# First layer of a hybrid decoder trunk: rows split in fp16 halves and transposed by DMA, and the first loop's order written out for four engines

## The chip, the cores and the metric

The kernel runs on one core of a Trainium2 chip. A time is the device time of one execution in microseconds (us). The kernel before has three such times, and one more execution was recorded by the profiler; all rows below and in the prediction are from that recording.

## The reference, cut to what matters

The program computes two residual layers over 2048 tokens of width 1024. Layer 0, which the change is in, mixes by gated linear attention (4 heads, a state per head that runs along the sequence); layer 1 mixes by dilated windows. Both also attend to a memory of 256 tokens.

```python
def reference(x, mem, mem_norm_w, norm_w, w_memkv, w_out, w_in_a, w_gate_up, b_gate,
              gla_norm_w, w_in_b, final_norm_w):
    mem_n = rmsnorm(mem, mem_norm_w)
    for i in range(DEPTH):                       # DEPTH = 2
        h = rmsnorm(x, norm_w[i])
        j = i // N_MIXERS
        if i % N_MIXERS == 0:
            mix, q_mem, gate = gla_mixer(h, w_in_a[j], w_gate_up[j], b_gate[j], gla_norm_w[j])
        else:
            mix, q_mem, gate = dilated_mixer(h, w_in_b[j])
        mem_o = memory_attention(q_mem, mem_n, w_memkv[i])
        branch = jnp.concatenate([mix, mem_o], axis=-1) * jax.nn.silu(gate)
        x = x + branch @ w_out[i]
    return rmsnorm(x, final_norm_w)
```

`gla_mixer` projects `h` to q, k (384 columns each), v (768), a gate of rank 16, the memory query (256) and the branch gate (1024).

## The kernel before, in words

The 2048 tokens are 16 blocks of 128 rows (`NB` = 16). A matrix product in f32 accuracy is made from fp16 halves: each operand is split into hi and lo = value - hi, and `mm3` (L181, L182, L183) adds hi*hi, hi*lo and lo*hi. `proj` runs `mm3` over 8 tiles of 128 along the width of 1024, so 24 matmuls for each 256 columns. The weight-like side has to have the width in its partitions, so each block of rows is first transposed.

The first layer has two loops over the 16 blocks, one after the other.

- **First loop** (pools of the context `c1`). `ga(b)` loads block b of x (L365), squares it for the norm (L160), scales it (L379), transposes its 8 tiles of 128x128 on TensorE (`split_T`, L168), and writes the result into `hT` as halves: hi by ScalarE (L384), lo by VectorE (L385), each in two pieces of 512 columns. `hT` is also stored to DRAM (`hT_d`, L388), since the second loop needs it again. `pre_a` to `pre_d` project block b to v, the gate and q, k and turn the gate into decays by exponentials; `gla1` transposes k and q (L525, L530), copies them to `kT` and `qT` on ScalarE (L527, L532) and makes the matrix A of the block (L538, masked at L540); `gla2` makes the outputs and the new state S, and stores the block to `og_d` (L571). At b = 1 the loop also writes the memory's rows, norm, transposes, keys and values of both layers (`mem_kv`); at b = 2 to 6 it loads and splits five weight tiles that the second loop needs (`load_w256`: load L136, conversion L140).
- **Second loop** (context `c2`). `a2_q` reads `hT` back (L637), projects the memory query and attends to the memory; `a2_gate` projects the 1024 gate columns and applies silu into `sg`; `a2_branch` reads `og` back (L663), multiplies into `sg` (L664, L666), transposes `sg` by `split_T`, and writes the halves to `bT` (L672, L673); `a2_out` multiplies `bT` by w_out's four tiles `wo0` to `wo3` and adds the residual (x1 is stored at L691); `a2_h2` makes the norm of the second layer, its halves in `stg` (L701, L702) and, for most blocks, transposes them by one DMA (`h2T<-stg`, L703). At a few blocks, `SUMS_AT`, `a2_sums` makes extra sums for the second layer (L719 to L732). Between the loops w_out's tiles are loaded, scaled and split (`load_w`, with `norm_scale` L113 to L124).

What sets the order: the program's text is handed to a scheduler, which puts every engine's instructions in an order of its own by a model of their costs. Each engine then runs its list in that order, and an instruction that must wait holds back all behind it on its engine. All loads, stores and DMA transposes are issued by SyncE (`SY`), so they too form one list, in which an issue that waits for its input holds back the issues behind it. A tile name has as many buffers as its pool says: `k1` has two of each name, `k2` one.

Of the kernel before, what the change touches and what calls it, by code (L numbers as in the profile page):

```python
# [16 lines left out]
P = 128  # L17
T = 2048
D = 1024
KT = 8  # L20
# [16 lines left out]
def trunk(ctx, tc, a, out):  # L37
# [318 lines left out]
    with ExitStack() as c1:  # L356
# [17 lines left out]
        def ga(b):  # L374
# [3 lines left out]
            r = rstd_of(rowss(xt, k2), 1, D)  # L378
# [11 lines left out]

        wv2, iv2 = lw1(1280, 272, s1)
        hs = [ga(0)]
        xts[1] = load_x(1)
        hs.append(ga(1))
# [48 lines left out]
        def pre_a(b, hT):  # L443
            v = tl(k1, [P, 768], F32, "v")
            p0 = bank(ps_mm)
            proj(p0[:, :272], hT, wv2, 0, 272)
            gl = gls[b % 2]
# [4 lines left out]
            A.activation(out=v[:, 512:768], in_=p0[:, :256], func=AF.Copy, scale=iv2)  # L452
            t = bank(ps_tr)
            PE.transpose(t[:96, :P], gl.bitcast(F32), ident)
            glT = tl(k2, [96, P], F32R, "glT")
            V.tensor_copy(glT, t[:96, :P])
            z = bank(ps_g)
            PE.matmul(z[:, :384], glT, wgu, start=True, stop=True)
            la = tl(k2, [P, 384], F32, "la")
# [4 lines left out]
                                   op1=ALU.subtract)  # L464
            bb = bank(ps_g)
            lah = tl(k2, [P, 384], F32R, "lah")
            lal = tl(k2, [P, 384], F32R, "lal")
            A.activation(out=lah, in_=la, func=AF.Copy)
            V.tensor_tensor(out=lal, in0=la, in1=lah.bitcast(F32), op=ALU.subtract)
            PE.matmul(bb[:, :384], tri, lah, start=True, stop=False)  # L470
            PE.matmul(bb[:, :384], tri, lal, start=False, stop=True)
            eb = tl(k1, [P, 384], F32, "eb")
            enb = tl(k1, [P, 384], F32, "enb")
            elb = tl(k1, [P, 384], F32, "elb")
            A.activation(out=enb, in_=bb[:, :384], func=AF.Exp, scale=-1.0)
            A.activation(out=eb, in_=bb[:, :384], func=AF.Exp)
            br = bank(ps_g)
            PE.matmul(br[:, :384], rev, lah, start=True, stop=False)
            PE.matmul(br[:, :384], rev, lal, start=False, stop=True)
            for h in range(HA):  # L480
                PE.matmul(br[:DK, 384 + 2 * h:386 + 2 * h], la[:, h * DK:(h + 1) * DK], ind, start=True, stop=True)
            A.activation(out=elb, in_=br[:, :384], func=AF.Exp)
            dec = tl(k1, [DK, 8], F32, "dec")
            A.activation(out=dec, in_=br[:DK, 384:392], func=AF.Exp)
            return hT, (v, eb, enb, elb, dec)

        def pre_b(hT, r):
            v = r[0]
            p1 = bank(ps_mm)
            proj(p1[:, 0:256], hT, wv0, 0, 256)  # L490
            A.activation(out=v[:, 0:256], in_=p1[:, 0:256], func=AF.Copy, scale=iv0)  # L491
            proj(p1[:, 256:512], hT, wv1, 0, 256)
            A.activation(out=v[:, 256:512], in_=p1[:, 256:512], func=AF.Copy, scale=iv1)
# [4 lines left out]
        def pre_c(hT, r):  # L498
            v, eb, enb, elb, dec = r
            p2 = bank(ps_mm)  # L500
            proj(p2[:, 0:256], hT, wk1, 0, 256)
            scaled(enb[:, 128:384], p2[:, 0:256], ik1)
            scaled(elb[:, 128:384], p2[:, 0:256], ik1)

        def pre_d(hT, r):
            v, eb, enb, elb, dec = r
            p3 = bank(ps_mm)
            proj(p3[:, 256:512], hT, wqk, 0, 256)
            scaled(enb[:, 0:128], p3[:, 384:512], iqk)
# [65 lines left out]
        for b in range(2):  # L575
            pres[b] = pre_a(b, hs[b])
# [1257 lines left out]
```

## Time and profile before

| | |
|---|---|
| median of 3 runs | 2574.38 us (2570.02 to 2577.67) |
| the profiled execution | 2568.94 us, its span 2567.2 us, granted clock 0.993 |
| TensorE busy (PE) | 2489.6 us, 97% of the span, 17033 matmuls |
| VectorE (DVE), ScalarE (ACT), GpSimd (POOL) busy | 1579.0, 1345.7, 579.2 us |
| share of the chain that ended last | PE 79%, DVE 6%, DMA 5%, issue 4%, ACT 4%, POOL 2% |

The span is the recorded part of one execution, from its first to its last instruction; what lies around it is 1.7 us here. "Busy" is summed over instructions of one engine, and PE's weight loads (PEld) run beside its matmuls. The chain that ended last is followed back from the last instruction through what each one waited for. In the trace the first layer's first loop runs from about 60 to 440 us, the second loop from about 500 to 912 us, and the rest, to the end, is the second layer.

### The profile page before, as it was taken

The numbers are of one execution on the slowest core, as the hardware profiler recorded it, in microseconds if no ns is written. First come the engines' busy times: TensorE is split into PE (matmuls) and PEld (weight loads), VectorE is DVE, ScalarE is ACT, GpSimd is POOL, SyncE is SP. The second block draws the span as 40 slices with busy tenths as digits, with TensorE's granted clock in tenths as the row PEclk, the third lists the DMA queues.
The fourth block names the chain that finished last, engine by engine and source line by source line (L and its number), as shares of the span: only waits on it lengthen the run. The fifth ranks groups of instructions, "written<-read, shape, count | busy, mean of one in ns | idle before, by whom it ended". The sixth has DMA issues, their size and how long they took to land.

```text
span 2567.2 us, 45017 instructions
## 1 busy us (share of the span) xinstructions
PE 2489.6 (97%) x17033; PEld 1673.3 (65%) x17033; DVE 1579.0 (62%) x3582; ACT 1345.7 (52%) x2944; POOL 579.2 (23%) x471
## 2 busy tenths in 40 slices
PE   7989999899999999999999999999999999998999
PEld 6979999788889844444444445555555555554898
DVE  7446444665776765756555455577676767768643
ACT  7346543644454544756555456565565656555322
POOL 0000000010210223454543112233232323323100
PEclk9999999999999999999999999999999999999999
DMA  6242111434544554567675323457474765648752
GB/s 213 84 133 95 54 67 52 133 112 110 163 133 128 146 185 121 143 165 185 169 183 141 127 56 92 114 149 175 121 183 125 174 150 147 177 116 219 234 179 101
DMA packets 563311, 356.55 MB, mean 139 GB/s; under 512 B 383554, under 2 KB 495636, under 8 KB 562708
## 3 DMA queue, kind: packets, MB, share of 16 engines
q1 hardware_dynamic: 563092, 353.66, 50.2%
q8 instruction: 133, 2.18, 0.3%
q14 instruction: 86, 0.70, 0.1%
HBM read 185.74 MB, written 95.86 MB: 110 GB/s over the span
## 4 chain that ended last, share of the span: by engine, by line
PE 79%; DVE 6%; DMA 5%; issue 4%; ACT 4%; POOL 2%; SPq 1%; DVEq 0%; POOLq 0%; ACTq 0%
PE ps_mm L181 15%; PE ps_mm L183 15%; PE ps_mm L182 15%; PE ps_x L181 6%; PE ps_x L182 6%; PE ps_x L183 6%; DMA mpt<-stg 1%; PE ps_o L183 1%; PE ps_o L181 1%; PE ps_o L182 1%; PE ps_g L181 1%; PE ps_g L182 1%; PE ps_g L183 1%; DMA h2T<-stg 1%; PE ps_tr L168 1%
## 5 line engine op out<-in xcount | busy, mean ns | idle before, releaser
L181 PE MATMUL ps_mm<-h2T,w 128*128 128x512 f16 x1112 | 422.9, 380 | 5.9 <-ACT w L851 4.9
L183 PE MATMUL ps_mm<-h2T,w 128*128 128x512 f16 x1112 | 422.6, 380 | 0.3 <-DVE w L855 0.3
L182 PE MATMUL ps_mm<-h2T,w 128*128 128x512 f16 x1112 | 422.7, 380 | 0.0
L181 PE MATMUL ps_mm<-w,hT 128*128 128x256 f16 (+1 forms) x1408 | 387.3, 275 | 3.2 <-ACT v L491 1.2
L182 PE MATMUL ps_mm<-w,hT 128*128 128x256 f16 (+1 forms) x1408 | 386.2, 275 | 0.0
L183 PE MATMUL ps_mm<-w,hT 128*128 128x256 f16 (+1 forms) x1408 | 385.0, 275 | 0.4 <-DVE hT L385 0.4
L183 PEld LDWEIGHTS <-w 128*128 128x128 f16 x1952 | 191.5, 98 | 233.2 <-issue 3.0
L181 PEld LDWEIGHTS <-w 128*128 128x128 f16 x1952 | 191.6, 98 | 216.7 <-ACT w L851 5.0
L182 PEld LDWEIGHTS <-w 128*128 128x128 f16 x1952 | 191.5, 98 | 216.4 <-issue 9.0
L175 POOL TENSOR_TENSOR ph<-pm,ph 128x512 f16<-128x512 f32 (+2 forms) x144 | 163.1, 1132 | 630.8 <-ACT ph L174 433.0
L181 PE MATMUL ps_x<-h2T,w 128*128 128x512 f16 x552 | 209.9, 380 | 1.4 <-DVE c L1079 1.4
L182 PE MATMUL ps_x<-h2T,w 128*128 128x512 f16 x552 | 210.0, 380 | 0.0
L183 PE MATMUL ps_x<-h2T,w 128*128 128x512 f16 x552 | 209.8, 380 | 0.0
L1268 ACT ACTIVATE pm<-pm,st,cols 128x256 f32<-128x256 f32 (+1 forms) x288 | 156.1, 543 | 73.8 <-DVE st L1261 73.1
L175 POOL TENSOR_TENSOR stg<-mp,stg 128x512 f16<-128x512 f32 x16 | 18.6, 1161 | 742.3 <-DMA ogd<-og 457.5
L181 PEld LDWEIGHTS <-hT 128*128 128x128 f16 x1408 | 138.7, 99 | 24.2 <-issue 5.5
L1257 DVE CUSTOM_DVE_ANT_0 pm<-ps_g,mw 128x256 f32<-128x256 f32 (+1 forms) x288 | 93.0, 359 | 99.6 <-PE ps_g L183 99.0
L182 PEld LDWEIGHTS <-hT 128*128 128x128 f16 x1408 | 138.7, 98 | 23.0 <-issue 4.4
L183 PEld LDWEIGHTS <-hT 128*128 128x128 f16 x1408 | 139.2, 99 | 17.9 <-DVE hT L385 0.7
L1217 ACT ACTIVATE rx<-rw 128x512 f16<-128x512 f32 x36 | 33.8, 940 | 114.8 <-DVE rw L1216 114.8
L1201 ACT ACTIVATE rx<-ps_mm 32x512 f32<-32x512 f32 x96 | 56.1, 584 | 57.8 <-PE ps_mm L183 24.6
L174 ACT ACTIVATE ph<-pm 128x512 f16<-128x512 f32 (+2 forms) x144 | 77.3, 537 | 4.5
(593 smaller groups left out, 5982.4 us busy)
## 6 DMA issues: line engine op xcount, KB each, us to landing
stg<-in_w_in_b SPq DMA_DIRECT2D x80, 256.0 KB
v<-vd SPq DMA_DIRECT2D x72, 256.0 KB
fb<-fd SPq DMA_DIRECT2D x24, 768.0 KB
od<-osb SPq DMA_DIRECT2D x68, 256.0 KB
og<-od SPq DMA_DIRECT2D x68, 256.0 KB
x<-in_x SPq DMA_DIRECT2D x32, 512.0 KB
stg<-in_w_in_b SPq DMA_DIRECT2D x24, 512.0 KB
vd<-vo SPq DMA_DIRECT2D x48, 256.0 KB
```

What stands on the lines that cost most here:

```text
L168: PE.transpose(t[:, (k - k0) * P:(k - k0 + 1) * P], src[:, k * P:(k + 1) * P], ident)
L174: A.activation(out=hi, in_=src, func=AF.Copy)
L175: G.tensor_tensor(out=lo, in0=src, in1=hi, op=ALU.subtract)
L181: PE.matmul(o, sh, mh, start=first, stop=False)
L182: PE.matmul(o, sh, ml, start=False, stop=False)
L183: PE.matmul(o, sl, mh, start=False, stop=last)
L1201: A.activation(out=X[r0:r0 + 32, :], in_=t[0:32, :], func=AF.Copy)
L1217: A.activation(out=fold(X.bitcast(F16)[:, 0:512], g), in_=perm(W, g), func=AF.Copy, scale=SQ)
L1257: V.tensor_tensor_reduce(out=pm[:, at:at + w * P], in0=s[:, at:at + w * P], in1=masks["mw" if w == 2 else "mf"], scale=1.0, scalar=NEG, op ...
L1268: A.activation(out=p_, in_=p_, func=AF.Exp, scale=sc, bias=st[:, jc + jj:jc + jj + 1], accum_out=st[:, ns + jc + jj:ns + jc + jj + 1])
```

## The change

Four edits, all in layer 0.

1. **Rows of 14 input blocks are transposed by DMA.** For b = 2 to 15, `ga_steps` takes the place of `ga`: the scaled rows are split before they are transposed, hi by one ScalarE instruction of 1024 columns (L405), lo by one VectorE instruction (L407), both into one tile `hl`, and one `dma_start_transpose` (L409) on SyncE's queue turns `hl` into `hT`. Blocks 0 and 1 keep `split_T`. The rows of block b+3 are now prepared in iteration b (before: of block b+2), and x of the block after that is loaded an iteration earlier than it was.
2. **The first loop is cut in pieces and its order written out.** Inside `tc.manual_schedule` the four engines PE, DVE, Activation and Pool (a tuple `MANUAL` of names) take the loop's instructions in the order of the text; SyncE's is still the scheduler's. Side work is held in generators (`ga_steps`, `mem_rows`, `w2_steps`), of which `tick` runs a step or two at fixed places. The memory's rows go to iterations 0 and 1; keys and values of layer 0 are loaded at b = 2 and made at b = 3 to 5; those of layer 1 are loaded at b = 11 and made at b = 14 and 15; the five weight tiles are loaded at b = 5 to 9, each converted in the iteration after.
3. **Rows of 15 branch blocks are transposed by DMA** in the second loop (blocks 0 to 14): hi by L864 on ScalarE, lo by L865 on VectorE into `hl`, and a DMA transpose (L866) into `bT`. `hl` and `og` are one buffer; there is a single one. `om` loses one of its two buffers.
4. w_out's norm: the square of the second half of each tile runs on VectorE.

```diff
+        def ga_steps(b):
+            xt = xts.pop(b)
+            if b + 1 < NB:
+                xts[b + 1] = load_x(b + 1)
+            hl = tl(k2, [P, 2, D], F16, "hl")
+            ss = tl(sp, [P, 1], F32, "ss")
+            A.activation(out=hl[:, 1].bitcast(BF16), in_=xt, func=AF.Square, accum_out=ss)
+            yield
+            r = rstd_of(ss, 1, D)
+            V.scalar_tensor_tensor(out=xt, in0=xt, scalar=r, in1=nw0, op0=ALU.mult, op1=ALU.mult)
+            yield
+            A.activation(out=hl[:, 0], in_=xt, func=AF.Copy, scale=sh0)
+            yield
+            V.scalar_tensor_tensor(out=hl[:, 1], in0=xt, scalar=sh0, in1=hl[:, 0], op0=ALU.mult, op1=ALU.subtract)
+            hT = tl(k1, [P, 2, KT, P], F16, "hT")
+            SY.dma_start_transpose(hT.rearrange("p a k n -> p (a k) n"), hl.rearrange("p a n -> p (a n)"))
+            SY.dma_start(hT_d[b], hT)
+            hTs[b] = hT
...
+        xts[2] = load_x(2)
+        for _ in ga_steps(2):
+            pass
...
+        c1.enter_context(tc.manual_schedule(engines={getattr(mybir.EngineType, e_) for e_ in MANUAL}))
+        kvr = w2r = None
         for b in range(NB):
-            S = gla2(b, pres[b][1], aqs[b], S)
-            if b + 2 < NB:
-                hT = ga(b + 2)
-            if b + 2 < NB:
-                pres[b + 2] = pre_a(b + 2, hT)
-            if b + 2 < NB:
-                pre_b(*pres[b + 2])
-            if b + 2 < NB:
-                pre_c(*pres[b + 2])
-            if b + 2 < NB:
-                pre_d(*pres[b + 2])
-            if b + 1 < NB:
-                aqs[b + 1] = gla1(b + 1, pres[b + 1][1])
-            if b == 1:
...
-                kvi = [mem_kv(i, memT, (stg, sga)) for i in range(2)]
-            if 2 <= b < 7:
-                c0 = 1552 if b == 2 else 1808 + (b - 3) * 256
-                w2.append(load_w256(w_in_a[:, c0:c0 + 256], invh0, wp, stg if b % 2 else sga))
+            n = blk_hT(b + 2) if b + 2 < NB else None
+            m = blk[b + 1] if b + 1 < NB else None
+            if b + 3 < NB:
+                act.insert(0, ga_steps(b + 3))
+            if b == 0:
+                act.append(mem_rows())
+            if b in (2, 11):
+                kvr = mem_load(b // 11)
+            if b == 3:
+                kvs = mem_steps(0, kvr, tl(wp, [P, 4, 512], F16, "w"))
+            if w2r is not None:
+                act.append(w2_steps(w2r))
+            w2r = w2_load(b - 5) if 5 <= b < 10 else None
+            S = gla_o(blk[b], S)
...
+            if n:
+                pre_gl(n)
+            gla_out(blk[b])
+            if n:
+                pre_v(n, 0)
+                pre_glT(n)
+                tick(2)
+                pre_v(n, 1)
+                pre_z(n)
+                pre_v_out(n)
...
+            if m:
+                gla_T(m)
+            tick(2)
+            if n:
+                pre_la(n)
+                pre_k(n)
+            if m:
+                gla_A(m)
+            tick(2)
+            if n:
+                pre_qk(n)
+                tick(2)
+                pre_eb(n)
+                pre_k_out(n, "enb")
+                pre_q(n)
+                tick(2)
+                pre_elb(n)
+                pre_k_out(n, "elb")
+                pre_qk_out(n)
+                pre_q_out(n)
...
         def a2_branch(b, om, sg, st):
-            og = tl(k2, [P, 768], F32, "og")
+            hl = tl(k2, [P, 2 * D], F16, "og")
+            og = hl.bitcast(F32)[:, 0:768]
...
             bT = tl(k2, [P, 2, KT, P], F16, "bT")
+            if b + 1 < NB:
+                A.activation(out=hl[:, 0:D], in_=sg, func=AF.Copy)
+                V.tensor_tensor(out=hl[:, D:2 * D], in0=sg, in1=hl[:, 0:D], op=ALU.subtract)
+                SY.dma_start_transpose(bT.rearrange("p a k n -> p (a k) n"), hl)
+                return bT
...
-                                  (stg, sga)[j % 2], "stg", ps_tr)))
+                                  (stg, sga)[j % 2], "stg", ps_tr, True)))
```

The pieces `pre_gl` to `gla_out` hold the instructions of `pre_a` to `pre_d`, `gla1` and `gla2`; `mem_steps` and `w2_steps` hold those of `mem_kv` and `load_w256`. From the end of the second loop on, PE, DVE and ACT have the same instructions in the same order as before.

Below, rows of the engines' lists, as the two programs have them: line, operation, output <- inputs, shape; numbers tell buffers of one name apart.

**First loop, PE and ACT, one iteration.** PE before, where a block's rows (`x`) are transposed between the last projection (`ps_mm`) and the matrix A (`ps_g<-qT,kT`):

```order
L182 LDWEIGHTS hT_435_2227
L182 MATMUL ps_mm_454_2384<-w1_256_151_370,hT_435_2227 128x256
L183 LDWEIGHTS hT_435_2227
L183 MATMUL ps_mm_454_2384<-w1_256_151_370,hT_435_2227 128x256
L168 MATMUL ps_tr_481_2526<-ident_1_82,x_431_2218 128x128 x4
L168 MATMUL ps_tr_482_2533<-ident_1_82,x_431_2218 128x128 x4
L538 MATMUL ps_g_460_2453<-qT_458_2449,kT_456_2442 128x128 x4
L555 MATMUL ps_g_470_2491<-v_393_1945,elb_404_1995 96x192 x2
```

PE after, at the matrix A (now L577):

```order
L182 LDWEIGHTS hT_413_2173
L182 MATMUL ps_mm_459_2478<-w1_512_145_349,hT_413_2173 128x256
L183 LDWEIGHTS hT_413_2173
L183 MATMUL ps_mm_459_2478<-w1_512_145_349,hT_413_2173 128x256
L577 MATMUL ps_g_460_2503<-qT_454_2465,kT_452_2458 128x128 x4
L181 LDWEIGHTS hT_413_2173
L181 MATMUL ps_mm_461_2509<-w1_256_151_370,hT_413_2173 128x256
```

The eight transposes of `x` are gone, and L577 now stands among the projections of the next block, behind that block's k projection (24 matmuls, of which the last stand in the rows) and the transposes of k and q. ACT before, between the v copy and the copy of `qT`:

```order
L491 ACTIVATE v_438_2243<-ps_mm_452_2306,cols_4_88 128x256
L527 ACTIVATE kT_456_2442<-ps_tr_455_2437 96x512
L460 ACTIVATE la_443_2279<-ps_g_442_2277 128x384
L461 ACTIVATE la_443_2279<-la_443_2279 128x384
L462 ACTIVATE la_443_2279<-la_443_2279,cols_4_88 128x384
L468 ACTIVATE lah_445_2285<-la_443_2279 128x384
L493 ACTIVATE v_438_2243<-ps_mm_452_2306,cols_4_88 128x256
L532 ACTIVATE qT_458_2449<-ps_tr_457_2444 96x512
```

ACT after, the same work:

```order
L497 ACTIVATE la_287_1310<-ps_g_286_1308 128x384
L498 ACTIVATE la_287_1310<-la_287_1310 128x384
L499 ACTIVATE la_287_1310<-la_287_1310,cols_4_88 128x384
L490 ACTIVATE v_275_1207<-ps_mm_279_1246,cols_4_88 128x256 x2
L564 ACTIVATE kT_289_1322<-ps_tr_288_1317 96x512
L569 ACTIVATE qT_291_1329<-ps_tr_290_1324 96x512
L405 ACTIVATE hl_283_1277<-x_236_974,cols_4_88 128x1024
L506 ACTIVATE lah_294_1338<-la_287_1310 128x384
```

Before, the copy to `kT` stood ahead of the three steps of `la`, and `qT` behind one copy of v; now both stand behind the three steps and both copies of v, and the split of the next rows (L405) follows.

**First loop, SyncE, around the loads of x.** Before, near the memory's keys and values (`kvd`, `kk`, `kl`, `vm`) and the first weight tile (L136):

```order
L225 DMA kl0_859_5141<-kvd_68_156 64x2x256
L136 DMA stg_372_1864<-in_w_in_a 128x4x256 x2
L227 DMA vm0_860_5143<-kvd_68_156 128x2x512
L365 DMA x_386_1920<-in_x 128x1024
L388 DMA hTd4_9_97<-hT_345_1631 128x2048
L215 DMA kvd_68_156<-w_321_1526 128x4x512
L365 DMA x_431_2218<-in_x 128x1024
```

After, one iteration with a weight tile (`stg<-in_w_in_a`, now L673), from the transpose of one block's rows to the next block's:

```order
L409 DMA_TRANSPOSE hT_537_3028<-hl_527_2970 128x16x128
L365 DMA x_569_3255<-in_x 128x1024
L410 DMA hTd10_15_103<-hT_537_3028 128x2048
L673 DMA stg_554_3157<-in_w_in_a 128x4x256 x2
L611 DMA ogd8_29_117<-og_565_3220 128x768
L409 DMA_TRANSPOSE hT_580_3315<-hl_570_3257 128x16x128
```

The load of x now has the transpose of the rows of the block before ahead of it, and no store or reload of the memory's keys; these stand in other iterations.

**Second loop, PE.** Before, the transposes of a branch block (`sg`) in the middle of the next block's memory query (`ps_mm<-w,hT`):

```order
L182 LDWEIGHTS hT_1322_9749
L182 MATMUL ps_mm_1323_9751<-w_371_1863,hT_1322_9749 128x256
L168 MATMUL ps_tr_1320_9735<-ident_1_82,sg_1301_9487 128x128 x4
L168 MATMUL ps_tr_1321_9742<-ident_1_82,sg_1301_9487 128x128 x4
L183 LDWEIGHTS hT_1322_9749
L183 MATMUL ps_mm_1323_9751<-w_371_1863,hT_1322_9749 128x256
```

After, the end of the same query, where the gate's first projection (another `w`) follows:

```order
L182 LDWEIGHTS hT_1299_9815
L182 MATMUL ps_mm_1300_9817<-w_499_2779,hT_1299_9815 128x256
L183 LDWEIGHTS hT_1299_9815
L183 MATMUL ps_mm_1300_9817<-w_499_2779,hT_1299_9815 128x256
L181 LDWEIGHTS hT_1299_9815
L181 MATMUL ps_mm_1313_9904<-w_542_3066,hT_1299_9815 128x256
```

No transposes stand in the query or between it and the gate. SyncE gets the transposes instead; after, at a block with sums:

```order
L902 DMA_TRANSPOSE h2T_824_4964<-stg_872_5181 128x16x128
L890 DMA x1d_37_125<-x_1066_7226 128x1024
L918 DMA a21d_69_157<-h2T_824_4964 128x4x128 x2
L866 DMA_TRANSPOSE bT_1074_7348<-og_1073_7344 128x16x128
L931 DMA S1d_70_158<-stg_872_5181 128x1024
L857 DMA og_1105_7706<-ogd7_28_116 128x768
L931 DMA S3d_72_160<-stg_873_5182 128x1024
L931 DMA S2d_71_159<-stg_872_5181 128x1024
L931 DMA S4d_73_161<-stg_873_5182 128x1024
L830 DMA hT_1139_8055<-hTd9_14_102 128x2048
```

Before, this stretch read the same without L866, and `og` of the next block (L857, before L663) stood ahead of the `x1d` store; the load now comes behind the transpose that reads the buffer it shares.

More of the change, by code (lines that the diff above doesn't have):

```diff
@@ L464, in pre_a @@
                                    op1=ALU.subtract)
-            bb = bank(ps_g)
[L466 to L472, printed above, removed]
@@ L485, in pre_a @@
[L485 to L493, printed above, removed]
+                PE.matmul(br[:DK, 384 + 2 * h:386 + 2 * h], d["la"][:, h * DK:(h + 1) * DK], ind, start=True,
+                          stop=True)
@@ new lines, in mem_load, with mem_steps @@
+        def mem_load(i):
+            ws_ = []
+            for j, sp_ in enumerate((stg, sga)):
+                w = tl(sp_, [P, KT, 256], F32, "stg")
+                SY.dma_start(w, a["w_memkv"][i, :, j * 256:(j + 1) * 256].rearrange("(k p) n -> p k n", p=P))
+                ws_.append(w)
+            return ws_
+        def mem_steps(i, ws_, kv):
+            invs = kvi[i]
+            for j, w in enumerate(ws_):
+                t = bank(ps_mm)
+                for m in range(2):
+                    for k in range(KT):
+                        ms = slice(m * P, (m + 1) * P)
+                        PE.matmul(t[:, m * 256:(m + 1) * 256], w[:, k, ms] if j == 0 else memT[:, k, ms],
+                                  memT[:, k, :] if j == 0 else w[:, k, :], start=k == 0, stop=k == KT - 1)
+                rm = tl(sp, [P, 1], BF16, "rb")
+                V.tensor_reduce(out=rm, in_=t, axis=AX.X, op=ALU.max, apply_absolute_value=True)
+                yield
+                tot = colsum(rm)
+                s = tl(sp, [P, 1], F32, "ws")
+                inv = col()
+                pow2(s, inv, tot, 2.0 ** -40, 2.0 ** 13)
+                invs.append(inv)
+                A.activation(out=kv[:, 2 * j, :], in_=t, func=AF.Copy, scale=s)
+                V.scalar_tensor_tensor(out=kv[:, 2 * j + 1, :], in0=t, scalar=s, in1=kv[:, 2 * j, :],
+                                       op0=ALU.mult, op1=ALU.subtract)
+                yield
+            SY.dma_start(kv_d[i].rearrange("j p n -> p j n"), kv)
@@ new lines, in trunk, with blk_hT @@
+        blk = [dict(b=b) for b in range(NB)]
+        def blk_hT(b):
+            blk[b]["hT"] = hTs.pop(b)
+            return blk[b]
+        for b in range(2):
+            pre_gl(blk_hT(b))
+            pre_glT(blk[b])
+            pre_z(blk[b])
+            pre_la(blk[b])
+            pre_eb(blk[b])
+            pre_elb(blk[b])
+        for b in range(2):
+            for j in range(2):
+                pre_v(blk[b], j)
+            pre_v_out(blk[b])
+        for b in range(2):
+            pre_k(blk[b])
+            for nm in ("enb", "elb"):
+                pre_k_out(blk[b], nm)
@@ new lines, in trunk, with tick @@
+        for b in range(2):
+            pre_qk(blk[b])
+            pre_q(blk[b])
+            pre_qk_out(blk[b])
+            pre_q_out(blk[b])
+        w2, wo = [], []
+        gla_T(blk[0])
+        gla_A(blk[0])
+        xts[2] = load_x(2)
+        for _ in ga_steps(2):
+            pass
+        memT = tl(s1, [P, KT, NMEM], F32, "stg")
+        kvi = [[], []]
+        act = []
+        def tick(k=1):
+            for _ in range(k):
+                if act:
+                    if next(act[0], 0) is not None:
+                        act.pop(0)
@@ L616, in trunk @@
+        next(kvs)
+        next(kvs, 0)
+        tick(20)
     ch = ctx.enter_context(ExitStack())
```

233 lines of the change are left out of this document (152 added, 81 removed).

## The prediction

> **What bounds the kernel now.** I read the page's busy times and its chain first, then the layer's stretches in a view by windows, then what PE waits for, then the chain's pieces in order of time.
>
> ```profile
> PE 2489.6 (97%) x17033; PEld 1673.3 (65%) x17033; DVE 1579.0 (62%) x3582; ACT 1345.7 (52%) x2944; POOL 579.2 (23%) x471
> PE 79%; DVE 6%; DMA 5%; issue 4%; ACT 4%; POOL 2%; SPq 1%; DVEq 0%; POOLq 0%; ACTq 0%
> ```
>
> PE is busy in 97% of the span and on 79% of the chain: work taken off PE is time, wherever PE is not waiting. Where it waits, the stretches tell (busy us of PE, PEld, DVE, ACT, POOL, then PE's granted clock, DMA share, GB/s):
>
> ```profile
> 60.00:150.00 90.00, 87.91 (x629) 77.88 (x628) 37.20 (x92) 28.47 (x77) 0.00 (x0) 1.00 0.28 95
> 150.00:165.00 15.00, 9.43 (x70) 7.64 (x68) 2.72 (x8) 7.29 (x16) 0.00 (x0) 0.77 0.61 193
> 165.00:440.00 275.00, 274.97 (x2350) 249.57 (x2349) 133.84 (x312) 143.93 (x364) 0.00 (x0) 1.00 0.18 67
> 460.00:505.00 45.00, 35.45 (x317) 30.06 (x315) 28.47 (x69) 32.97 (x62) 2.36 (x2) 0.96 0.49 155
> 505.00:600.00 95.00, 94.12 (x907) 84.51 (x905) 57.88 (x130) 40.63 (x94) 9.82 (x8) 1.00 0.38 102
> 600.00:750.00 150.00, 142.29 (x1356) 126.01 (x1354) 111.48 (x226) 73.83 (x155) 30.68 (x24) 1.00 0.54 144
> 750.00:850.00 100.00, 99.95 (x954) 90.13 (x952) 57.77 (x134) 44.29 (x95) 9.09 (x8) 1.00 0.42 112
> 850.00:912.00 62.00, 55.51 (x485) 45.77 (x484) 49.64 (x93) 31.68 (x64) 12.81 (x10) 0.94 0.57 166
> ```
>
> First loop, 165 to 440: PE idles 0.03 us of 275. There is nothing to win from a better order, only from less work. Before it, 60 to 165, PE idles 2.1 + 5.6 us. Between the loops (460 to 505) it idles 9.5 us. In the second loop it is full at 505 to 600 and 750 to 850, and not in the two stretches with sums, 600 to 750 (7.7 us idle) and 850 to 912 (6.5 us).
>
> **Transposes off PE.** Chain pieces (start, us, what): the A matrix of three blocks' spacing in the first loop, four of a block's eight transposes there, one projection matmul, and the transposes of two blocks of the second loop.
>
> ```profile
> 319.47 0.89 PE ps_g L538 x8
> 343.12 0.44 PE ps_tr L168 x4
> 343.55 0.89 PE ps_g L538 x8
> 750.22 0.11 PE ps_o L183
> 755.58 0.87 PE ps_tr L168 x8
> 781.80 0.87 PE ps_tr L168 x8
> ```
>
> Four transposes take 0.44 us of PE and eight 0.87; a block takes 343.55 - 319.47 = 24.1 us in the first loop and 781.80 - 755.58 = 26.2 us in the second. First loop: 14 blocks x 0.87 = **-12.2 us**, all on the bound engine. Second loop: 15 x 0.87 = 13.1 us are taken away, but by the windows only about 9 of the 15 blocks lie where PE is full: **-7.8 us**. In the sums stretches the time lies in a chain that does not hold the transposes (h2T's DMA, the sums, then silu and the next norm), so I take nothing there; the ends are -13 and -3, the latter if the new DMA delays the sums.
>
> The halves are cheaper on the other engines: one instruction of 1024 columns takes the place of two of 512 (group rows: total, mean ns; idle before).
>
> ```profile
> L701 ACT ACTIVATE stg<-sg 128x1024 f16<-128x1024 f32 x13 | 13.7, 1055 | 5.5 <-DVE sg L697 4.0 <-DMA kl<-kvd 1.4
> L702 DVE TENSOR_TENSOR stg<-sg,stg 128x1024 f16<-128x1024 f32 x13 | 15.8, 1219 | 0.0
> L672 ACT ACTIVATE bT<-ps_tr 128x512 f16<-128x512 f32 x32 | 18.0, 593 | 71.0 <-PE ps_tr L168 66.5 <-PE ps_x L183 4.5
> L673 DVE TENSOR_TENSOR bT<-ps_tr,bT 128x512 f16<-128x512 f32 x32 | 21.4, 686 | 17.6 <-ACT bT L672 17.4
> ```
>
> The same operations on the same shapes stand already at L701 and L702: ACT 1.06 for 2 x 0.59, DVE 1.22 for 2 x 0.69 a block. Neither bounds a full stretch (DVE 58 of 100, ACT 44), so this counts nothing.
>
> **Do the DMA transposes land in time?** A transpose of this shape, 128x2048 in fp16, is there already (h2T). Its pieces in the chain, and SyncE's queue (start, length of issue):
>
> ```profile
> 669.13 4.55 DMA h2T<-stg
> 857.25 3.64 DMA h2T<-stg
> 641.05 1.62 SPq L703 DMA_TRANSPOSE h2T<-stg  x1
> 651.99 0.33 SPq L732 DMA_DIRECT2D S3d<-stg  x1
> 780.93 0.32 SPq L691 DMA_DIRECT2D x1d<-x  x1
> 795.37 0.32 SPq L637 DMA_DIRECT2D hT<-hTd  x1
> ```
>
> It lands 3.6 to 4.6 us after its issue, and holds the queue for 1.6. In the second loop the output of a block ends where x1d is stored (780.9) and the next output starts once the gates are done, about where the next hT load is issued (795.4): 14 us. The new halves are ready 1.06 + 1.22 = 2.3 us in, and land by 6.9: 7 us to spare, hidden. At a block with sums the transpose stands behind the a21d store and ahead of S1d on SyncE, so it is issued near 646 and out by 647.6; S3d, at 652 now, isn't held up, and the load of og behind it has until the next branch.
>
> In the first loop the block would take 24.1 - 0.87 = 23.2 us. The k and q transposes of the PE list stand about half an iteration in; ACT then has the copies below, ending near 15.5 us; the hi copy (L405) and the lo (L407) follow, ready at about 18.7 us, landed by 23. The first reader is the first projection of the next iteration, which stands behind that iteration's outputs and state update, some 4 us in, so near 27.5 us. About 5 us are spare. The issues behind it on SyncE (the next x, the hT store, a weight tile) have an iteration of lead each.
>
> **The stall at 150 to 165.** Wait row of PE (total, times, longest), the chain's piece, the queue, and two windows:
>
> ```profile
> PE ps_tr L454 <- ACT rs L154: 5.6, 1, 5.6
> 150.74 7.79 DMA x<-in_x
> 148.50 1.14 SPq L136 DMA_DIRECT2D stg<-in_w_in_a  x2
> 161.00:164.00 3.00, 3.00 (x16) 2.18 (x15) 0.79 (x2) 0.59 (x2) 0.00 (x0) 0.52 0.00 0
> 164.00:167.00 3.00, 3.00 (x29) 2.62 (x28) 0.00 (x0) 1.63 (x3) 0.00 (x0) 1.00 0.00 0
> ```
>
> x of a block is issued behind the memory's keys and a weight tile, lands 7.8 us later, and PE waits 5.6 us; then 3 us run at a clock of 0.52, which loses 1.4. The Trainium skill, "TensorE: Matmul & The Clock Gate", Part 1, has it that PE falls to half clock after an idle window of some 3.4 us and comes back after a busy one; the trace agrees, with 0.52 behind a wait of 5.6 us, and the waits that I price below are too short for that rule to add to them. In the new order the x loads are issued an iteration earlier, and the memory's work stands elsewhere: the 2.1 + 5.6 + 1.4 = **-9.1 us** go. What is late next is the memory's work itself, whose matmuls stand between full projections.
>
> **What the fixed order adds.** An engine in fixed order waits where the scheduler would have put something else. The one place in each iteration is the A matrix (L577) behind the copies to kT and qT on ACT, now behind la and v:
>
> ```profile
> 359.22 0.49 ACT L460 ACTIVATE la<-ps_g 128x384 f32<-128x384 f32 x1 [1.66 <-PE ps_g L458]
> 360.30 0.61 ACT L462 ACTIVATE la<-la,cols 128x384 f32<-128x384 f32 x1
> 361.97 0.46 ACT L493 ACTIVATE v<-ps_mm,cols 128x256 f32<-128x256 f32 x1
> 356.97 0.59 ACT L527 ACTIVATE kT<-ps_tr 96x512 f32<-96x512 f32 x1
> 362.84 0.59 ACT L532 ACTIVATE qT<-ps_tr 96x512 f32<-96x512 f32 x1 [0.42 <-PE ps_tr L530]
> 344.98 0.72 DVE L540 COPY_PREDICATED AT<-cmask,ps_g 128x512 f32<-128x512 int32 x1
> ```
>
> From the gate matmul (L495) to qT: three la steps 0.49, 0.55 (the middle one taken between the two shown) and 0.61, two v copies 0.92, kT and qT 1.18: 3.75 us, with the hops between engines some 3.9. PE has meanwhile the gate matmul itself 0.2, the transposes 0.87 and the k projection, 24 matmuls of 0.11 each, 2.6: 3.7. So it waits about 0.2 us, in 14 blocks **+2.8**. Bounds: 0, if the v copies run while la waits for its input; 1.0 us each (14), if DVE's part (glT) makes the gate late too. Five weight conversions add a column sum on PE behind ACT's squares, 0.2 each, **+1**. The head (block 0's A matrix and mask with no projection between: qT 0.59, mask 0.72, hops) **+2**, the tail (blocks 14 and 15 with no next projections; layer 1's memory matmuls cover part) **+2.5**, other small ones **+0.8**; ends 0 and 10 for these together. Sum **+9.1**.
>
> **Between the loops.** Two waits of PE and one load:
>
> ```profile
> PE ps_tr L120 <- DVE rb L118: 4.0, 2, 2.9
> PE ps_g L286 <- ACT wo L116: 3.7, 1, 3.7
> 487.70 6.21 DMA stg<-in_w_out
> ```
>
> PE waits for w_out's column sums (4.0) and for ACT, which is at w_out's squares (3.7). With half of the squares on DVE and the column sums behind more gate matmuls in the PE list these shrink; but the last two loads of w_out stand behind the first block's transpose on SyncE, so one may come late by its 6.2 us. I take **-4**, between -9.5 (all idle goes) and +5.
>
> **Sum.** -12.2 - 9.1 + 9.1 - 4 - 7.8 = -24.0 us. The second layer has the same orders and is taken as unchanged. The profiled run, 2568.9, would be 2545; it lies 5.4 us under the median of 2574.4, so against the median **2550**.
>
> **The rivals.**
> - *All of PE's saving counts* (0.15). The sums blocks are shortened too (-5.2 more) and the gap between the loops closes (-5.5): 2550 - 10.7 = 2539. For it: PE is the engine with the most busy time even at 600 to 750, 95%. Against it: 7.7 us of idle there belong to another chain.
> - *The fixed order eats the gain of the first loop* (0.20). 0.8 us more per block at the A matrix, x 14 = 11: 2561. For it: the margin there, 3.7 against 3.9, is gone with one more hop between engines; the scheduler's order left 0.03 us of idle in 275, so any difference is a loss.
> - *No change that can be measured* (0.08): that loss, and w_out's load late by its 6 us and not hidden, with no gain between the loops: 2550 + 11 + 10 = 2571. The difference that a measurement of this kernel can tell is about 0.3%, 7.7 us.
> - *The DMA transposes come late* (0.07), the other side. In the first loop every us of landing beyond the 5 us spare costs PE one us a block, x 14. It turns the result slower than before by more than 7.7 us once it costs 24 + 7.7 = 32 us, 2.3 us a block: a landing of 4 + 5 + 2.3 = 11 us. At 12 us it is 2550 + 3 x 14 = 2592. For it: the x load took 7.8 us behind other transfers at a DMA share of 0.61. Against it: 3.6 and 4.6 us for the same shape at shares of 0.54 to 0.57, and the first loop's share is 0.18.
>
> The Trainium skill, "VectorE: DVE Perf Modes", in The three transpose paths and the rules behind it, speaks for this rival: it gives 1309 ns for a 128x128 transpose through the DMA crossbar against 390 ns on TensorE, and advises TensorE wherever PSUM will do as the destination. Worked out from that page as an estimate, 16 tiles would take 20.9 us, 12 us late in each of 14 blocks and 9 us in each of 15, some 300 us in all, near 2855. The trace disagrees for this shape, by its 3.64 us for all 16.
>
> **How the numbers follow.** The likeliest case, 0.50, is the sum, with 2541 to 2559 from its inner bounds. The range reaches from below the first rival to the edge of the third, 2534 to 2570. Faster 0.50 + 0.15 + 0.20 = 0.85, same 0.08, slower 0.07.
>
> **What would show it.** Right: A matrices 23.2 to 23.5 us apart in the first loop, blocks of the second without sums 25.4; a PE wait for qT of some 0.2 us per block; no PE wait at hT or bT for a DMA; a clock of 1.00 at 150 to 165; about the same time in the sums stretches, with more idle in them. Wrong: a row of PE at pre_gl or a2_out waiting for a DMA transpose, waits at L577 near 1 us, or a larger gap between the loops.

## The result and the profile after

| | before | after |
|---|---|---|
| median | 2573.97 us (2570.02 to 2577.67, 4 runs) | 2550.41 us (2546.75 to 2552.74, 4 runs) |
| profiled execution | 2568.94 us, span 2567.2 | 2548.53 us, span 2546.7 |

The ratio is 0.9907, 95% interval 0.9887 to 0.9928. The forecast was 2550, range 2534 to 2570. The total came as forecast, but not by the forecast's terms: the first loop gave half of what it should. The two profiles are 20.5 us apart, and what the medians' 23.6 have beyond that is less than the runs of one kernel differ by (7.7 us before, 6.0 after). The profile's page after (span; busy time and share):

```profile
span 2546.7 us, 44545 instructions
PE 2470.1 (97%) x16801; PEld 1654.8 (65%) x16801; DVE 1578.6 (62%) x3561; ACT 1332.7 (52%) x2907; POOL 578.6 (23%) x471
```

PE has 232 instructions less and is busy 19.5 us less, against a span that is 20.5 us shorter: the idle time of PE shrank by 1.0 us only.

Two landmarks carry the rest. The last start in the row of `sg` transposes stands for the end of layer 0 on PE. These last eight are not a branch block, as the expectations below have it: they are block 15's rows for the second layer (`xn`, L911, whose buffer has the name `sg` too; on PE in both kernels). Ahead of them PE waits for a weight of layer 1 (4.3 us, before 4.9) and runs its first matmuls. The outputs of block 15 tell the same: they end at 880.7 instead of 899.0, 18.3 us earlier. The last A matrix (block 15) ends the first loop's recurrence, almost. Group rows with durations, first and last start; of before, then after:

```profile
L168 PE MATMUL ps_tr<-ident,sg x152: 272/273/327, 498.9 to 912.9; 128*128 128x128 f32 x152
L538 PE MATMUL ps_g<-qT,kT x128: 273/275/275, 62.9 to 450.9; 96*128 96x128 f32 x128
```

```profile
L168 PE MATMUL ps_tr<-ident,sg x32: 272/273/273, 520.8 to 895.0; 128*128 128x128 f32 x32
L577 PE MATMUL ps_g<-qT,kT x128: 275/275/377, 62.2 to 434.8; 96*128 96x128 f32 x128
```

Layer 0 ends at 895.0 instead of 912.9: **-17.9 us**. What comes behind it is 1654.3 us of span before and 1651.7 after, though the engines have the same order there. In the profiles of this study that remainder lies between 1651.7 and 1659.7, whatever was changed in layer 0. So a landmark in layer 0 tells a few us apart where a total cannot, and I use it below. It is read from one execution too: in four profiles with the same first loop (the kernel after and experiments 4 to 6) the last A matrix starts between 432.1 and 434.7, so a difference of 2 us by itself says little.

The A matrix comes 16.1 us earlier, but that is not yet the first loop's gain. Behind it, after still has the second half of layer 1's memory keys and values (7.15 us of PE from 439.97 to 447.12); before had 3.1 us of the second loop's first query ahead of it (447.17 to 450.28). At equal work the first loop gives about 16.1 - 7.15 - 3.1 = **-5.9**, and what follows to the end of layer 0 gives **-12.0**. Forecast were -12.2 for the first loop and -11.8 for the rest.

In the first loop the rows that a DMA transposes come in time, as forecast; in the second, PE waits for two branch blocks (experiment 5). SyncE's queue (issue of the transpose, issue of the store that waits for it to land) and the first reader on PE:

```profile
274.03 1.83 SPq L409 DMA_TRANSPOSE hT<-hl  x1
280.13 0.33 SPq L410 DMA_DIRECT2D hTd<-hT  x1
283.48 0.28 PE L181 MATMUL ps_mm<-w,hT 128*128 128x272 f16 x1
```

Landed after 6.1 us at most (4.3 in the iteration before), with 3.4 to 5 us to spare. Chain pieces of two A matrices, and two stretches (columns as in the forecast's windows):

```profile
247.94 1.13 PE ps_g L577 x8
271.69 1.13 PE ps_g L577 x8
```

```profile
62.00:113.00 51.00, 46.40 (x349) 42.30 (x350) 21.70 (x45) 21.54 (x62) 0.00 (x0) 0.90 0.15 47
248.00:414.00 166.00, 166.00 (x1393) 148.98 (x1394) 88.24 (x200) 95.43 (x240) 0.00 (x0) 1.00 0.37 109
```

A block of the first loop takes 23.75 us where it has a weight tile beside it (24.35 before) and 23.52 where it has none (24.09 before, 23.2 forecast), and the A matrix itself takes 1.13 instead of 0.89. PE is still full there. At 62 to 113 it now idles 4.6 us, at a clock of 0.90: a stall that before did not have at this place (0.3 us idle from 62 to 110).

The kernel after also loads x of block 2 twice, by `ga(1)` (L377) and again at L734; no wait of PE in its profile goes to that.

### The profile page after: what moved, and what is told of

Same layout as the page of the kernel before. It is cut to its first block, busy times and chain, and to the rows that moved or that the text cites. A ratio compares the mean times of both kernels' runs of the same rounds, so it can differ in the third digit from the quotient of the medians.

```text
span 2546.7 us, 44545 instructions
## 1 busy us (share of the span) xinstructions
PE 2470.1 (97%) x16801; PEld 1654.8 (65%) x16801; DVE 1578.6 (62%) x3561; ACT 1332.7 (52%) x2907; POOL 578.6 (23%) x471
## 4 chain that ended last, share of the span: by engine, by line
PE 79%; DVE 7%; DMA 6%; issue 3%; ACT 3%; POOL 1%; SPq 1%; DVEq 0%; POOLq 0%; ACTq 0%
PE ps_mm L183 15%; PE ps_mm L181 15%; PE ps_mm L182 15%; PE ps_x L183 6%; PE ps_x L181 6%; PE ps_x L182 6%; DMA mpt<-stg 1%; PE ps_mm L652 1%; PE ps_g L181 1%; PE ps_g L183 1%; PE ps_g L182 1%; PE ps_o L181 1%; PE ps_o L183 1%; PE ps_o L182 1%; DMA h2T<-stg 1%
```

## The experiments

Each is one edit to the kernel after, unless it says otherwise. "Layer 0 ends" is the last start of the row of `sg` transposes, 895.0 in the kernel after and 912.9 before.

**1. What the input transposes cost on PE.** The rows of blocks 2 to 15 go back to TensorE, in the written order.

```diff
-            A.activation(out=hl[:, 0], in_=xt, func=AF.Copy, scale=sh0)
+            ...                            # hT, and emit for its halves
             yield
-            V.scalar_tensor_tensor(out=hl[:, 1], in0=xt, ...)
-            SY.dma_start_transpose(hT..., hl...)
+            split_T(xt, KT, emit)          # 8 transposes, halves in two pieces
```

> Changed kernel with the input blocks' rows transposed on TensorE again (8 transposes, halves in two pieces), the written order kept. Theory (the gain of the first loop is TensorE time, 0.87 us a block): the last branch transposes, which end layer 0 on TensorE, come 14 x 0.87 = 12 us later than the changed kernel's 895 us, so at about 907, and the time is near 2562. Rival (the gain came with the written order, and the transposes were hidden in it): less than 4 us later, near 2552.

Measured: 2611.61 us (2609.85 to 2614.1), ratio to the kernel before 1.0151 (1.0136 to 1.0166); layer 0 ends at 948.8. What PE waited for:

```profile
PE ps_tr L168 <- ACT kT L568: 27.4, 13, 2.1
PE ps_tr L168 <- DVE qs L575: 6.6, 12, 0.6
```

Both expectations missed. In a fixed order the place decides: right behind the transposes of k and q, those of x wait for the PSUM bank that the copies of k and q hold, and PE waits with them. So the edit was repeated one step later, behind the A matrix:

```diff
             yield
+            yield
             split_T(xt, KT, emit)
```

> Changed kernel with the input blocks' rows transposed on TensorE again, but one step later in the written order than in the first attempt: behind the A matrix and not straight behind the transposes of k and q. In the first attempt a block took 27.3 us against 23.7, since the transposes waited for a PSUM bank that the copies of k and q held (27.4 us in all on kT, 6.6 on qs). Theory (that wait was the place's, not the transposes'): blocks about 23.7 + 0.9 = 24.6 us apart, layer 0 ends 12 to 14 us behind the changed kernel's 895, at 907 to 909, time near 2563. Rival (ScalarE and VectorE cannot take the eight halves copies in any fixed place): blocks 26 us or more apart, layer 0 ends past 925.

Measured: 2561.79 us (2560.33 to 2564.46), ratio 0.995 (0.9935 to 0.9965); layer 0 ends at 901.2. Two A matrices of it:

```profile
247.36 1.16 PE L582 MATMUL ps_g<-qT,kT 96*128 96x128 f32 x8
271.87 1.16 PE L582 MATMUL ps_g<-qT,kT 96*128 96x128 f32 x8
```

A block with a weight tile takes 24.51 us against 23.75, 0.76 more; one without takes 24.40 against 23.52, 0.88 more. For 5 and 9 of them that is 11.7. The transposes are worth what their PE time is (0.87 was forecast). At the end of layer 0 only 6.2 show: the extra step also moved the memory's transposes on, and the stall of 62 to 113 went (25.5 us for that block, 31.0 in the kernel after); the block before it is 1.6 shorter, which differs from run to run (experiment 6). So the block's length is the theory's, and the end is earlier than both expectations.

**2. The stall that took the old one's place.** In the first iteration PE waits for the second norm of the memory's rows, which stands behind the outputs of q and k on VectorE. Of after: that wait (and below it that of the memory's keys and values, L652), the two norms, the clock.

```profile
PE ps_tr L633 <- DVE stg L628: 3.6, 1, 3.6
PE ps_mm L652 <- DVE elb L530: 2.2, 2, 1.1
```

```profile
85.14 1.28 DVE L628 SCALAR_TENSOR_TENSOR stg<-stg,rs,w 128x1024 f32<-128x1024 f32 x1
92.55 1.28 DVE L628 SCALAR_TENSOR_TENSOR stg<-stg,rs,w 128x1024 f32<-128x1024 f32 x1
```

```profile
93.00:96.00 3.00, 2.02 (x8) 2.05 (x9) 1.52 (x2) 0.00 (x0) 0.00 (x0) 0.50 0.00 0
96.00:99.00 3.00, 3.00 (x11) 3.00 (x10) 0.00 (x0) 0.84 (x4) 0.00 (x0) 0.50 0.00 0
```

3.6 us of wait, and then 5 us at half clock. The edit makes both norms in one step:

```diff
+            for m in range(2):
+                V.scalar_tensor_tensor(out=mts[:, m, :], in0=mts[:, m, :], scalar=rs[m], in1=mnw, ...)
+            yield
             for m in range(2):
-                V.scalar_tensor_tensor(out=mt, in0=mt, scalar=r, in1=mnw, ...)
-                yield
```

> Changed kernel with the norms of both memory row blocks made in one step, ahead of the memory's transposes. Theory (in the first iteration TensorE waits 3.6 us for the second norm, then runs some 5.5 us at half clock, and that ate the gain from the old stall): that wait goes, the clock stays 1.00 at 90 to 100 us, layer 0 ends 5 to 6.5 us earlier than 895, at 889 to 890. Rival (the wait moves on to another place, since VectorE is late there anyway): layer 0 ends within 2 us of 895.

Measured: 2546.67 us (2544.52 to 2554.53), ratio 0.9903 (0.9883 to 0.9923). The same stretch of its profile, and its landmarks:

```profile
93.00:96.00 3.00, 3.00 (x26) 2.58 (x25) 1.38 (x4) 0.42 (x3) 0.00 (x0) 1.00 0.50 173
L577 PE MATMUL ps_g<-qT,kT x128: 274/275/378, 62.4 to 427.1; 96*128 96x128 f32 x128
L168 PE MATMUL ps_tr<-ident,sg x32: 272/273/273, 515.2 to 891.2; 128*128 128x128 f32 x32
```

The wait and the half clock are gone, the block takes 25.2 instead of 31.0 us (5.8), and the last A matrix comes 7.7 us earlier (the head's part, 1 to 2 us, differs from run to run). Layer 0 ends 3.8 earlier, between the two expectations. About 2 us are given back between the loops (block 0's outputs end 5.6 earlier), and as much in the second loop, where the memory attention on PE waits 4.2 us for ScalarE's rs, against 1.7 in the kernel after.

**3. The A matrix behind la and v.**

```diff
                 pre_z(n)
-                pre_v_out(n)
...
             if m:
                 gla_T(m)
+            if n:
+                pre_v_out(n)
```

> Changed kernel with the two copies of v placed behind the copies of kT and qT on ScalarE. Theory (the A matrix starts 0.24 us late in each block since qT stands behind la and v): qT is there 0.9 us earlier, A's eight passes take 0.89 again and follow the projection at once, blocks 23.3 to 23.5 us apart instead of 23.5 to 23.75, layer 0 ends 2.5 to 3.5 us earlier, at about 892. Rival (the 0.24 us are a switch between fp16 and f32 weights, not a wait): nothing moves, 895.

Measured: 2550.18 us (2548.53 to 2553.81), ratio 0.9901 (0.9885 to 0.9918); layer 0 ends at 892.9. Waits of the weight loads between 60 and 440 us, of after and of this kernel, and two of its A matrices:

```profile
PEld ps_g L577 <- ACT qT L569: 5.4, 16, 1.0
PEld L105 <- DVE rb L685: 1.1, 5, 0.2
```

```profile
PEld ps_g L577 <- ACT qT L569: 1.9, 2, 1.0
PEld L105 <- DVE rb L685: 2.3, 5, 0.5
```

```profile
386.38 0.89 PE ps_g L577 x8
409.65 0.89 PE ps_g L577 x8
```

The wait was one for qT and not a switch of weight types: it goes in 14 blocks, 3.5 us in all, and A takes 0.89 again. Blocks without a weight tile take 23.28 us instead of 23.52. In the five with one, the column sum (L105) waits longer instead, and they stay at 23.75. The 2.1 us at the landmark are too few to count by themselves; the waits show the gain.

**4. The branch transposes.** All 15 back on PE (`if b + 1 < 0` in place of `if b + 1 < NB`).

> Changed kernel with all 15 branch blocks transposed on TensorE again. Theory (only the 9 blocks outside the sums pay): layer 0 ends 7.8 us later, at 903, time near 2558. Rivals: all 15 pay, 13 us later, 908; or, since from the fifth to the last block the changed kernel gained only 2.4 us on the kernel before, new waits ate most of it and it ends less than 4 us later.

Measured: 2569.68 us (2564.98 to 2571.67), ratio 0.9983 (0.9974 to 0.9993).

```profile
L168 PE MATMUL ps_tr<-ident,sg x152: 272/273/330, 493.2 to 909.2; 128*128 128x128 f32 x152
```

14.2 us later, more than the 7.8 expected. Yet it is not that the sums blocks pay: the outputs of blocks 5 to 9 end 8.2 to 9.5 us later than in the kernel after, so only 1.0 comes from block 5 to block 9; blocks 10 to 13 add 4.0, where four times 0.87 is 3.5. The large piece, 8.2, is there by block 5: 0.8 of it before the second loop, 5.2 for six blocks of transposes, 1.4 in more idle time of PE; the rest is open. Nor is it what the transposes are worth against the kernel before: from block 5's outputs to the landmark this kernel takes 4.0 us longer than the kernel before, with the same work on PE (the second row is of before).

```profile
635.40:909.20 273.80, 260.81 (x2415) 227.07 (x2414) 194.58 (x396) 131.68 (x274) 48.66 (x39) 0.99 0.52 139
643.10:912.90 269.80, 258.72 (x2415) 227.31 (x2414) 193.77 (x396) 132.13 (x274) 48.94 (x39) 0.99 0.50 141
```

What costs these 4.0 was not isolated. `om` has one buffer here and two before, and PE waits 3.4 us for the memory attention's `mp`, 1.4 before.

**5. Block 0 alone.** In the kernel after PE waits 4.1 us for the first branch block's transpose. This puts that block on PE (`if 0 < b < NB - 1`).

> Changed kernel with branch block 0 alone transposed on TensorE. Theory (between the loops TensorE waits 4.1 us for that block's DMA transpose): the wait goes for 0.9 us of transposes, layer 0 ends 3 us earlier, at 892. Rival (w_out's tiles are late there anyway): the output waits for them instead, layer 0 ends at 895 or later.

Measured: 2555.61 us (2551.32 to 2557.84), ratio 0.9923 (0.9908 to 0.9938); layer 0 ends at 898.7. Waits between the loops, of after and then of this kernel:

```profile
PE ps_o L181 <- DMA bT<-og: 4.1, 1, 4.1
```

```profile
PE ps_mm L181 <- DVE ws L124: 3.7, 1, 3.7
```

One wait takes the place of the other, as the rival had it, and the end is 3.7 us later.

**6. The squares on VectorE.** Taken out of the kernel after:

```diff
-                                  (stg, sga)[j % 2], "stg", ps_tr, True)))
+                                  (stg, sga)[j % 2], "stg", ps_tr)))
```

> Changed kernel with both squares of w_out's tiles on ScalarE again. Forecast's step (the squares on VectorE shorten the waits between the loops, -4 with the column sums): layer 0 ends 3 to 5 us later than 895, at 898 to 900. Rival (between the loops TensorE waits for the first DMA transpose and w_out's tiles in any case): layer 0 ends within 2 us of 895.

Measured: 2549.69 us (2549.52 to 2553.81), ratio 0.9911 (0.9896 to 0.9926); layer 0 ends at 893.5. And put alone into the kernel before:

> Kernel before with only the squares of w_out's second halves on VectorE. Forecast's step: PE's waits for column sums and for ScalarE between the loops (4.0 and 3.7 us) shrink, layer 0 ends 3 to 5 us before 912.9. Rival (w_out's loads set the pace there): within 2 us of 912.9.

Measured: 2571.11 us (2568.61 to 2575.6), ratio 0.9997 (0.9987 to 1.0006). The landmark rows, without the squares and then with them alone:

```profile
L168 PE MATMUL ps_tr<-ident,sg x32: 272/273/331, 520.9 to 893.5; 128*128 128x128 f32 x32
```

```profile
L168 PE MATMUL ps_tr<-ident,sg x152: 272/273/330, 496.8 to 913.4; 128*128 128x128 f32 x152
```

Nothing either way beyond what single profiles differ by: this edit is worth 0 in both kernels.

**7. Both DMA transposes without the written order.** The kernel before, with the rows split and transposed as in the kernel after (`om` loses its second buffer as there), and the scheduler's order.

```diff
+            if b > 1:
+                A.activation(out=hl[:, 0], in_=xt, func=AF.Copy, scale=sh0)
+                V.scalar_tensor_tensor(out=hl[:, 1], in0=xt, scalar=sh0, in1=hl[:, 0], ...)
+                SY.dma_start_transpose(hT..., hl...)
...
+            if b + 1 < NB:
+                A.activation(out=hl[:, 0:D], in_=sg, func=AF.Copy)
+                V.tensor_tensor(out=hl[:, D:2 * D], in0=sg, in1=hl[:, 0:D], op=ALU.subtract)
+                SY.dma_start_transpose(bT..., hl)
```

> Kernel before with both kinds of rows transposed by DMA and nothing else: the scheduler orders the first loop, the memory's work stays at b = 1, w_out's squares stay on ScalarE. Theory (the gain is TensorE time, the written order gives as much as it takes): layer 0 ends 12 + 8 = 20 us before the kernel before's 912.9, at about 893, time 2552 to 2556. Rival (the written order is needed to have the rows ready an iteration early, without it the projections wait for the DMA transposes, some us in each of 14 blocks): layer 0 ends at 905 or later, time 2565 or more.

Measured: 2562.82 us (2559.56 to 2565.14), ratio 0.9956 (0.9939 to 0.9973). Its landmarks and two of its waits:

```profile
L548 PE MATMUL ps_g<-qT,kT x128: 272/275/422, 65.4 to 451.0; 96*128 96x128 f32 x128
L168 PE MATMUL ps_tr<-ident,sg x32: 272/273/273, 533.1 to 905.2; 128*128 128x128 f32 x32
PE ps_tr L464 <- DVE gl L461: 5.9, 1, 5.9
PE ps_g L548 <- ACT eb L486: 4.8, 10, 1.1
```

In the first loop it gains nothing (last A matrix at 451.0, 450.9 before): what the transposes leave, waits for VectorE and ScalarE take, in the scheduler's order; PE idles 15.6 us there, 7.6 before. The 5.9 are the old stall, still at its place (151 us). The new waits, as the 4.8 in ten pieces, lie mostly in the blocks with a weight tile, which take 25.0 to 26.0 us instead of 24.4; blocks without one take 23.64 instead of 24.09, so that half of the 0.87 shows there. The end is the rival's, but not for its reason: the projections wait for a DMA transpose once, 1.4 us. From the last A matrix on it gains 7.7, of which 6.9 are there by the end of block 5's outputs. So it is the written order, with the memory's work and the weight tiles moved and the rows ready an iteration earlier, that turns the first loop's free PE time into time; which of these does it was not separated.

**8. How late a transpose may land.** Each input transpose is issued two and three times into the same tile.

```diff
-            SY.dma_start_transpose(hT..., hl...)
+            for _ in range(3):
+                SY.dma_start_transpose(hT..., hl...)
```

> Changed kernel with each of the 14 input transposes issued three times into the same tile. Theory (one lands 4.3 to 6.1 us after its issue, they go one behind the other, and the first reader comes 9.4 us after the issue, so 5 us at most were spare): three land after some 13 us, 3.5 us late, in 13 blocks some 45 us: layer 0 ends near 940. Rival (the further ones overlap with the first or the reader has more slack): layer 0 ends below 900.

> Changed kernel with each of the 14 input transposes issued twice. With three, TensorE waited 45.8 us for the rows in 10 blocks. Theory (9.4 us from issue to reader, one takes 4.3 to 6.1): two land after 8.6 to 10, so a wait of 1 us at most in some blocks, layer 0 ends within 8 us of 895. Rival (no slack was left by the first): about half of what three cost, 930.

Measured, one run each: 2560.2 us with two, layer 0 ends at 901.9; 2621.4 us with three, layer 0 ends at 963.5. PE's waits with two and with three, and with three one block's queue; then the stretch from the third A matrix to the last, with one and with three:

```profile
PE ps_mm L181 <- DMA hT<-hl: 4.8, 3, 2.1
```

```profile
PE ps_mm L181 <- DMA hT<-hl: 45.8, 10, 6.4
301.80 1.88 SPq L410 DMA_TRANSPOSE hT<-hl  x1
316.51 0.34 SPq L411 DMA_DIRECT2D hTd<-hT  x1
```

```profile
112.80:433.90 321.10, 317.87 (x2584) 285.25 (x2583) 151.74 (x346) 154.36 (x403) 0.00 (x0) 1.00 0.37 109
112.40:501.70 389.30, 340.27 (x2584) 294.37 (x2583) 151.75 (x346) 154.60 (x403) 0.00 (x0) 0.93 0.49 122
```

Three land after 14.7 us. The waits sum to 45.8, near the 45 expected (in 10 blocks, not 13), but the end moves by 68.5, past the 940 expected: in the stretch shown PE idles 45.8 us more (49.0 against 3.2), and is busy 22.4 us more for the same 2584 matmuls, at a clock of 0.93 instead of 1.00. Two cost 6.9, within the 8 expected, and nearly nothing in most blocks. So the rival of late transposes is real as a mechanism, with its price too low: some 1.5 us for each us of waiting. The kernel after has room for about one more transpose's length.

**9. Both repairs of the first loop together** (2 and 3).

> Changed kernel with both repairs of the first loop: memory norms in one step, copies of v behind those of kT and qT. Theory (two waits at different places, they add): the A matrix of the last block comes 7.7 + 4.3 = 12 us earlier than the changed kernel's 433.9, at 422; layer 0 ends 3.8 + 2.1 = 6 us earlier, at 889, time near 2546. Rival (the two repairs meet on ScalarE and VectorE in the first iteration): A of the last block not before 425, layer 0 ends at 891 or later.

Measured: 2543.77 us (2539.96 to 2546.74), ratio to the kernel before 0.9883 (0.9867 to 0.99).

```profile
L577 PE MATMUL ps_g<-qT,kT x128: 273/275/377, 61.5 to 424.1; 96*128 96x128 f32 x128
L168 PE MATMUL ps_tr<-ident,sg x32: 272/273/273, 510.3 to 886.4; 128*128 128x128 f32 x32
```

The last A matrix is 10.7 us earlier than in the kernel after and layer 0 ends 8.6 us earlier (some 2 us of both are again the head's part). The A matrix comes between the two expectations, the end before both. It is the fastest of this study; its interval touches the kernel after's (0.9887 to 0.9928), so the landmark shows the gain and the totals only agree with it.

## Why the prediction was right, step by step

- **Input transposes, -12.2.** Right: 0.76 or 0.88 us a block in experiment 1, 11.7 in all. That PE is full, so that its time is the price, held; that a free slot on PE turns into time whatever the order, did not (experiment 7).
- **The old stall, -9.1.** The step that failed. The x loads are on time and the old wait is gone, but the forecast itself named what is late next, "the memory's work itself, whose matmuls stand between full projections", and gave it no price. It cost 3.6 us of wait and the half clock behind it, 5.8 together (experiment 2); the memory's keys and values wait a further 2.2 us for a PSUM bank. So 8.0 of the 9.1 were paid again.
- **The fixed order, +9.1.** The wait at the A matrix was forecast at 0.2 us, and was 0.24, 3.5 instead of 2.8 in all, at the place and for the reason named (experiment 3). The column sums of weight tiles were forecast at +1 and waited 1.1. The head, the tail and the small ones (+5.3) no run isolates; of rows of waits, 1.7 us for the masked A (AT) and 1.4 for qT where no projection stands between belong there.
- **Between the loops, -4, and the second loop, -7.8.** Together -12.0, as the sum has it, but not where the sum has it: -10.0 are there by the end of block 5's outputs, at equal work, and -2.0 come behind it (269.8 us to the landmark before, 267.8 after; rows below). Up to there PE idles 4.0 less (13.6 before, 9.6 after), which is the size of the first term, though not for its reason: the squares on VectorE are worth nothing (experiment 6), and PE now waits 4.1 us for the first block's transpose and 0.7 for the second's. Such a row the forecast had named as a sign of being wrong. Six blocks of transposes are 5.2 more. That the sums blocks give next to nothing was forecast: from block 5 to block 9 it is 1.0. Blocks 10 to 13 were counted in full, 3.5, and give 1.7; they take 25.8 us each and not 25.4. PE idles 1.4 us there, where before it idled 0.05, on transposes of the memory attention that share the queue. So that the two terms add up is in part luck.
- **The total.** -5.9 and -12.0 in layer 0, and -2.6 behind it in the profiles, -20.5, against the forecast's -24.0. The medians differ by 23.6, which is nearer to the forecast than the explained part is. That rest can't be put down to an instruction: the remainder behind layer 0 differed by 8 us among kernels that are equal there.

From the last A matrix to the end of block 5's outputs, and blocks 10 to 13; before, then after (the rest of before stands in experiment 4). In the first stretch before has 3.1 us less to do and after 7.15 more, as said above:

```profile
450.12:643.10 192.98, 179.38 (x1682) 159.25 (x1681) 116.66 (x268) 94.51 (x206) 16.72 (x14) 0.99 0.43 118
753.90:859.00 105.10, 105.05 (x1010) 94.78 (x1008) 62.22 (x141) 46.99 (x100) 9.09 (x8) 1.00 0.42 112
```

```profile
433.95:627.20 193.25, 183.66 (x1693) 163.18 (x1694) 123.78 (x288) 92.03 (x195) 17.24 (x14) 0.99 0.51 132
627.20:895.00 267.80, 252.64 (x2343) 219.60 (x2342) 196.58 (x387) 131.67 (x265) 47.95 (x39) 0.99 0.66 160
737.00:840.40 103.40, 102.01 (x978) 91.11 (x976) 61.91 (x138) 47.22 (x97) 9.08 (x8) 1.00 0.63 134
```

Of the rivals, the one in which the fixed order eats the first loop's gain came half true, by the memory's rows and not by the A matrix, and the medians don't show it.

On the clock: behind the 3.6 us wait of the kernel after PE runs at 0.50 for 5 us, and in experiment 8 waits of 45.8 us come with 22.4 us of slower matmuls. Behind the 3.7 us wait of the kernel before, for ACT at w_out's squares, the clock stays at 1.00 (473 to 476 us), so a wait of this length can end either way. I had counted waits at their length in the rival of late transposes, and had called all waits in the sum too short to slow the clock, though one of them is those 3.7 us. The Trainium skill, "TensorE: Matmul & The Clock Gate", Part 1, has half clock after an idle window of some 3.4 us. The waits of 3.6 and 5.6 us agree with it; the one of 3.7 us shows that the length alone does not decide.

## What to carry to other kernels

Work that is taken off the engine that bounds becomes time only if the order lets the engine use the slot: the same transposes gave nothing in sum in the scheduler's order and 0.8 to 0.9 us a block in one written by hand, while back on PE at a bad place they cost 3.6 a block. When a stall is removed by moving work, price the moved work's own first wait, and count a wait of several us on PE with the slow clock behind it. Where totals scatter by as much as the terms of a sum, compare a landmark inside the changed part, and look up which instruction it is: two tiles here share one buffer's name.

## What was not expected of the hardware

DMA transposes are made of many small packets. The page's line on packets, before and then after:

```profile
DMA packets 563311, 356.55 MB, mean 139 GB/s; under 512 B 383554, under 2 KB 495636, under 8 KB 562708
```

```profile
DMA packets 623771, 372.23 MB, mean 146 GB/s; under 512 B 443890, under 2 KB 555972, under 8 KB 623172
```

29 transposes add 60336 packets of under 512 B, some 2081 each for half a megabyte. In the full blocks 10 to 13 of the second loop the DMA engines' share rises from 0.42 to 0.63, while the bytes rise from 112 to 134 GB/s.
